# Four of the first layer's weight subtractions issued on GpSimd instead of VectorE

## The chip, the cores and the metric

The kernel runs on one core of a Trainium2 chip. The metric is the device time of one launch in microseconds (us). A core has five engines with instruction queues of their own, each worked through in order: TensorE (PE in the profile, its weight loads PEld), VectorE (DVE), ScalarE (ACT), GpSimd (POOL) and SyncE (SP), which here only starts DMA transfers.

## The reference

Two layers of a bidirectional encoder over 272 tokens (16 meta tokens and 256 others) of width 1024. Each layer normalises its input, multiplies it by one wide matrix, runs retention and attention beside each other on the parts, merges them, and closes with a squared-ReLU MLP:

```
u = rms_norm(h, norm_mix_pre[l])
proj = u @ w_in[l]
q_r, k_r, v_r, g_r, q_a, k_a, v_a, gate_r, gate_a = split(proj)
y_r = retention_branch(q_r, k_r, v_r, g_r, log_decay, pad) @ w_ret_o[l]
y_a = attention_branch(q_a, k_a, v_a, attn_sink[l], pad) @ w_att_o[l]
mix = (sigmoid(gate_r) * y_r + sigmoid(gate_a) * y_a) @ w_mix_o[l]
h = h + rms_norm(mix, norm_mix_post[l])
u = rms_norm(h, norm_ff_pre[l])
h = h + rms_norm(square(relu(u @ w_ff1[l])) @ w_ff2[l], norm_ff_post[l])
```

All is in 32-bit floats. What matters here is the second line, in layer 0.

## The kernel before

The weights come in 260 units of 128 x 1024 floats (512 KB), used in the order in which the program names them. Units 0 to 3 are a special start ("leads": the first four value projections v_r). After them every unit goes the same way (`unit`, from L119): SP fetches it into `raw` (three buffers in rotation, so the DMA for unit n+3 starts when unit n's `raw` has been read by all its readers). ACT rounds it to the matmul's format, `wh` (L131, four buffers). DVE subtracts, `wl = raw - wh` (L132, four buffers), the low part. PE then makes three products for each of eight 128-row slices (`mm3`): `wh` with the activations' high part (L136), `wh` with their low part (L137), `wl` with the high part (L138). So a unit is 24 matmuls of 272 columns, and the third of them is the first that needs `wl`.

The units around the change, all of layer 0, are:

| unit | what it projects | buffers in the rows and the order (raw, wh, wl) |
|---|---|---|
| 4, 5 | values of heads 4 and 5 | wl_296, wl_326 |
| 6 | k_a, the attention keys | raw_113, wh_429, wl_430 |
| 7 | q_a 0, attention queries | raw_475, wh_477, wl_478 |
| 8 | values of head 6 | raw_522, wh_524, wl_525 |
| 9 | q_a 1 | raw_555, wh_557, wl_558 |
| 10 | values of head 7 | raw_602, wh_604, wl_605 |
| 11 | q_a 2 | raw_635, wh_637, wl_638 |
| 12, 13 | v_a, q_a 3 | wl_689, wl_721 |

Between them stand the uses of the products. `value_r` (L416) scales a value product by the norm's factor on DVE (`vt`, L424; two buffers in turn), lets POOL copy its 16 meta columns into a padded tile (`pads`, L427), and defers `centre`: four short PE products of `vt` (L431) and one of `pads` (L432), put into PE's queue in the middle of a later unit, after its fifth slice (`flush` in `product`). For head 6 they stand in the middle of unit 9. `key_a` rotates k_a on DVE (L389 to L392), splits it on ACT (`ka`, four instructions, L449) and DVE (`kal`, L451). `query_a` rotates q_a on DVE, then ACT writes its high part (`qa`, L459, two instructions), DVE its low part (L93, two), and POOL a scaled copy of its meta columns (L465, two).

The order of instructions on each engine is set by the framework's scheduler from its own estimate. The kernel bends it with `tc.issue_after(ins)`: what is traced in that block on the same engine as `ins` goes behind `ins`. `held` is a table from unit number to such instructions, read in `unit`; with an entry that is a POOL instruction only a POOL instruction of the unit is moved.

Of the kernel before, what the change touches and what calls it, by code (L numbers as in the profile page):

```python
# [41 lines left out]
def encoder(ctx: ExitStack, tc: tile.TileContext, order, w, h_in, gains, dec, decm, sink, sinkm, tabs, mats, esel, masks, rel, relm, grow, out):  # L42
    nc = tc.nc
    V, A, PE, G = nc.vector, nc.scalar, nc.tensor, nc.gpsimd
    mul, add, sub, mn = ALU.mult, ALU.add, ALU.subtract, ALU.min
# [27 lines left out]
    def bank(tag, shape=None):  # L73
        t = psum.tile([P, 512], F32, tag=tag, name="ps_" + tag, bufs=BANKS[tag])
        if shape is None:
            return t
        n = int(np.prod(shape))
        v = t[:, :n]
        if len(shape) == 2:
            v = v.rearrange("p (a b) -> p a b", a=shape[0])  # L80
        elif len(shape) == 3:
            v = v.rearrange("p (a b c) -> p a b c", a=shape[0], b=shape[1])
        return v
# [5 lines left out]
    def f(t):  # L89
        return t.bitcast(F32)  # L90
# [13 lines left out]
    count = {"load": 0}  # L104
    raws = []
    held = {}

    def fetch(parts=1):
        i = count["load"]
        count["load"] += 1  # L110
        raw = ring.tile([P, D], F32, tag="raw", name="raw", bufs=3)
        n = D // parts
        cuts = [slice(j * n, (j + 1) * n) for j in range(parts)]
        raws.append((raw, cuts))
        for c in cuts:
            nc.sync.dma_start(raw[:, c], w[i][:, c])
            yield

    def unit(*name):  # L119
        i = len(order)  # L120
        order.append(name)
        if not raws:
            list(fetch())
        raw, cuts = raws.pop(0)
        wh = ring.tile([P, D], F32R, tag="wh", name="wh")
        wl = ring.tile([P, D], F32R, tag="wl", name="wl")
        for c in cuts:
            with ExitStack() as later:
                for ins in held.get(i, ()):
                    later.enter_context(tc.issue_after(ins))  # L130
                A.activation(wh[:, c], raw[:, c], AF.Copy)  # L131
                V.tensor_tensor(out=wl[:, c], in0=raw[:, c], in1=f(wh[:, c]), op=sub)  # L132
        return wh, wl

    def mm3(ps, ah, al, bh, bl, first=True, last=True):
# [6 lines left out]
    def flush():  # L142
        while deferred:
            deferred.pop(0)()

    def product(x, c0, tag, *name):
        wh, wl = unit(*name)
        ps = bank(tag, [T])
        for k in range(KD):
            sl = slice(k * P, (k + 1) * P)  # L150
            ins = mm3(ps[:, c0:], wh[:, sl], wl[:, sl], x[0][:, k, c0:], x[1][:, k, c0:], k == 0, k == KD - 1)
            if k == LAG and deferred:
                with tc.issue_after(ins.ins):
                    flush()
            yield ins, ps

    def proj(x, c0, tag, *name):
        for _, ps in product(x, c0, tag, *name):
            pass
        return ps  # L160
# [177 lines left out]
    def fourfold(x):  # L338
        return x.unsqueeze(1).to_broadcast([x.shape[0], 4, 16])
# [23 lines left out]
    for l in range(DEPTH):  # L363
# [52 lines left out]
        def value_r(hh):  # L416
            q, m = hh // 4, hh % 4
            if m == 0:
                tpv[q] = bank("s", [4, P]), [bank("t") for _ in range(2)]
            tpm, tps = tpv[q]  # L420
            vt = ready.get(hh)
            if vt is None:
                vt = two.tile([P, T], F32, tag="t1", name="vt")
                last = V.scalar_tensor_tensor(out=vt, in0=early.pop(0) if early else proj(u, 0, "a", "v_r", hh), scalar=-0.5, in1=rb, op0=mul, op1=mul)  # L424
                scaled.append(last.ins)
            mine = vtm[:, m]
            G.tensor_copy(mine[:, :, 16 * (m % 2):16 * (m % 2) + 16], fourfold(vt[:, 0:16]))  # L427

            def centre():
                for c in range(2):  # L430
                    PE.matmul(tps[c][:, m * P:(m + 1) * P], vt[:, 16 + c * P:16 + (c + 1) * P], mat["cen"], start=True, stop=True)  # L431
                PE.matmul(tpm[:, m], mine, mat["cen"], start=True, stop=True)  # L432
                if m == 3:
                    for c in range(2):
                        A.activation(vr[:, c, q * 512:(q + 1) * 512], tps[c], AF.Copy)
                    A.activation(vm[:, 4 * q:4 * q + 4], tpm, AF.Copy)
                    for r in odds:
                        low = vm[r, 4 * q:4 * q + 4]
                        V.tensor_tensor(out=low, in0=tpm[r], in1=f(low), op=sub)

            deferred.append(centre)
            if early:
                flush()
# [23 lines left out]
        for hh in range(5):  # L467
            value_r(hh)
# [4 lines left out]
        for i in range(3):  # L473
            value_r(5 + i)
            query_a(i)
# [85 lines left out]
        if l == 0:  # L561
# [6 lines left out]
            for c in range(4):  # L568
                V.tensor_tensor(
                    out=pmblk.rearrange("p (t c g k) -> p t c g k", t=4, c=4, g=2)[:, :, c],  # L570
                    in0=mat["blk"].rearrange("p (t g k) -> p t g k", t=4, g=2),
                    in1=pm[:, 0:16].unsqueeze(1).unsqueeze(1).to_broadcast([P, 4, 2, 16]),
                    op=mul,
# [166 lines left out]
        for m2 in range(4):  # L740
            wh, wl = unit("att_o", m2)
            for i in range(2):
                m = 2 * m2 + i
                ps = bank(wide(), [T])
                for k in range(4):
                    sl = slice((4 * i + k) * P, (4 * i + k + 1) * P)
                    mm3(ps[:, c0:], wh[:, sl], wl[:, sl], ao[:, 0, k, c0:], ao[:, 1, k, c0:], k == 0, k == 3)
                stt(tha[m][:, c0:], tha[m][:, c0:], 1.0, ps[:, c0:], op0=add)
# [47 lines left out]
        if l == 0:  # L796
            def ff2():
                for m in range(KD):
                    ps = bank(wide(), [T])
                    for q in range(4):  # L800
                        wh, wl = unit("ff2", m, q)
                        for k in range(KD):
                            sl = slice(k * P, (k + 1) * P)
                            mm3(ps[:, c0:], wh[:, sl], wl[:, sl], fs[q][0][k][:, c0:], fs[q][1][k][:, c0:], q == 0 and k == 0, q == 3 and k == KD - 1)
                    yield m, ps

            update = leave(l, 3, c0, ff2(), e2)
# [180 lines left out]
```

## Time and profile before

| | |
|---|---|
| median of three runs | 868.79 us (868.16 to 870.78) |
| the profiled execution's own time | 872.21 us |
| its span, first to last instruction | 870.4 us |
| PE busy | 852.1 us, 98% |
| DVE, ACT, POOL busy | 603.2, 559.6 and 49.9 us |
| granted TensorE clock, mean of the span | 0.996 of full |

Read it so: PE has work nearly all the time, so only what leaves PE idle, or slows its clock, can be won or lost. The start up to about 5.7 us, when the first weights land, is not touched by the change. What remains is small, and it has to be looked for by place, not in the averages: in the list of what PE waited for, in the timeline of the stretch from 18 to 45 us, and in the granted clock by stretch.

### The profile page before, as it was taken

The numbers are of one execution on the slowest core, as the hardware profiler recorded it, in microseconds if no ns is written. First come the engines' busy times: TensorE is split into PE (matmuls) and PEld (weight loads), VectorE is DVE, ScalarE is ACT, GpSimd is POOL, SyncE is SP. The second block draws the span as 40 slices with busy tenths as digits, with TensorE's granted clock in tenths as the row PEclk, the third lists the DMA queues.
The fourth block names the chain that finished last, engine by engine and source line by source line (L and its number), as shares of the span: only waits on it lengthen the run. The fifth ranks groups of instructions, "written<-read, shape, count | busy, mean of one in ns | idle before, by whom it ended". The sixth has DMA issues, their size and how long they took to land.

```text
span 870.4 us, 16670 instructions
## 1 busy us (share of the span) xinstructions
PE 852.1 (98%) x6514; PEld 819.3 (94%) x6514; DVE 603.2 (69%) x1113; ACT 559.6 (64%) x1034; POOL 49.9 (6%) x113
## 2 busy tenths in 40 slices
PE   9899999999999999999999999999999999999997
PEld 9899999999989999999989999999999999998885
DVE  7889888778768655444469898888776675554544
ACT  7448887666568777444355588886755498783432
POOL 2112220000000000000000122200000000000000
PEclk9999999999999999999999999999999999999999
DMA  8544344445545655556544544444466367666661
GB/s 294 190 123 136 118 135 131 129 155 173 169 143 171 193 173 183 178 175 186 174 121 146 155 129 154 137 139 137 121 197 198 113 214 204 196 200 192 189 193 69
DMA packets 41407, 142.15 MB, mean 163 GB/s; under 512 B 5360, under 2 KB 6256, under 8 KB 41328
## 3 DMA queue, kind: packets, MB, share of 16 engines
q1 hardware_dynamic: 40896, 140.43, 52.1%
q8 instruction: 51, 0.84, 0.4%
q10 hardware_dynamic: 432, 0.66, 0.2%
q14 instruction: 28, 0.23, 0.1%
HBM read 140.02 MB, written 1.05 MB: 162 GB/s over the span
## 4 chain that ended last, share of the span: by engine, by line
PE 81%; DVE 10%; ACT 6%; issue 1%; DMA 1%; POOL 0%; SPq 0%; DVEq 0%; ACTq 0%; POOLq 0%
PE ps_a L136 12%; PE ps_a L137 12%; PE ps_a L138 12%; PE ps_s L138 5%; PE ps_s L137 5%; PE ps_s L136 5%; PE ps_t L136 4%; PE ps_t L137 4%; PE ps_t L138 4%; DVE wl L132 3%; PE ps_a L849 2%; PE ps_s L849 2%; PE ps_s L848 2%; PE ps_a L848 2%; PE ps_a L850 2%; PE ps_s L850 2%
## 5 line engine op out<-in xcount | busy, mean ns | idle before, releaser
L132 DVE TENSOR_TENSOR wl<-raw,wh 128x1024 fp32r<-128x1024 f32 x256 | 312.8, 1223 | 198.9 <-ACT wh L131 197.3
L131 ACT ACTIVATE wh<-raw 128x1024 fp32r<-128x1024 f32 x256 | 269.9, 1058 | 203.1 <-PE ps_a L137 61.6
L136 PE MATMUL ps_a<-uh,wh 128*128 128x272 f32 (+1 forms) x912 | 265.8, 292 | 2.8 <-ACT uh L242 2.8
L138 PE MATMUL ps_a<-uh,wl 128*128 128x272 f32 (+1 forms) x912 | 259.3, 284 | 0.3 <-DVE wl L132 0.3
L137 PE MATMUL ps_a<-ul,wh 128*128 128x272 f32 (+1 forms) x912 | 259.3, 285 | 0.0
L136 PEld LDWEIGHTS ps_a<-uh,wh 128*128 128x128 f32 x912 | 172.7, 189 | 4.7 <-ACT uh L242 3.2
L137 PEld LDWEIGHTS ps_a<-ul,wh 128*128 128x128 f32 x912 | 172.5, 189 | 0.9
L138 PEld LDWEIGHTS ps_a<-uh,wl 128*128 128x128 f32 x912 | 172.4, 189 | 0.7 <-DVE wl L132 0.7
L138 PE MATMUL ps_s<-uh,wl 128*128 128x272 f32 (+1 forms) x184 | 52.0, 283 | 0.3 <-DVE wl L132 0.3
L137 PE MATMUL ps_s<-ul,wh 128*128 128x272 f32 (+1 forms) x184 | 52.0, 282 | 0.0
L136 PE MATMUL ps_s<-uh,wh 128*128 128x272 f32 (+1 forms) x184 | 52.0, 283 | 0.0
L136 PE MATMUL ps_t<-uh,wh 128*128 128x272 f32 (+1 forms) x152 | 43.2, 284 | 1.3 <-ACT uh L242 1.3
L137 PE MATMUL ps_t<-ul,wh 128*128 128x272 f32 (+1 forms) x152 | 43.1, 284 | 0.0
L138 PE MATMUL ps_t<-uh,wl 128*128 128x272 f32 (+1 forms) x152 | 42.8, 282 | 0.0
L138 PEld LDWEIGHTS ps_s<-uh,wl 128*128 128x128 f32 x184 | 34.6, 188 | 0.5 <-DVE wl L132 0.5
L136 PEld LDWEIGHTS ps_s<-uh,wh 128*128 128x128 f32 x184 | 34.8, 189 | 0.0
L137 PEld LDWEIGHTS ps_s<-ul,wh 128*128 128x128 f32 x184 | 34.7, 189 | 0.0
L136 PEld LDWEIGHTS ps_t<-uh,wh 128*128 128x128 f32 x152 | 28.6, 188 | 1.5 <-ACT uh L242 1.5
L137 PEld LDWEIGHTS ps_t<-ul,wh 128*128 128x128 f32 x152 | 28.6, 188 | 0.1
L138 PEld LDWEIGHTS ps_t<-uh,wl 128*128 128x128 f32 x152 | 28.6, 188 | 0.0
L97 DVE TENSOR_TENSOR fl<-ft,fh 128x272 fp32r<-128x272 f32 (+1 forms) x64 | 27.6, 433 | 1.0 <-ACT fh L96 0.9
L96 ACT ACTIVATE fh<-ft 128x272 fp32r<-128x272 f32 (+1 forms) x64 | 27.1, 424 | 1.7
(308 smaller groups left out, 1948.3 us busy)
## 6 DMA issues: line engine op xcount, KB each, us to landing
raw<-in_w SPq DMA_DIRECT2D x256, 512.0 KB, 3.7
leads<-in_w SPq DMA_DIRECT2D x6, 256.0 KB, 5.3
tab<-in_tabs SPq DMA_DIRECT2D x2, 544.0 KB, 6.5
h<-in_h_in SPq DMA_DIRECT2D x3, 272.0 KB, 5.1
out<-yt SPq DMA_DIRECT2D x3, 256.0 KB, 2.1
leads<-in_w ACTq DMA_DIRECT2D x2, 256.0 KB, 3.8
gj<-in_grow SPq DMA_DIRECT2D x1, 512.0 KB, 5.5
mats<-in_mats SPq DMA_DIRECT2D x1, 320.0 KB, 7.2
```

What stands on the lines that cost most here:

```text
L96: A.activation(xh, x, AF.Copy)
L97: V.tensor_tensor(out=xl, in0=x, in1=f(xh), op=sub)
L131: A.activation(wh[:, c], raw[:, c], AF.Copy)
L132: V.tensor_tensor(out=wl[:, c], in0=raw[:, c], in1=f(wh[:, c]), op=sub)
L136: PE.matmul(ps, ah, bh, start=first, stop=False)
L137: PE.matmul(ps, ah, bl, start=False, stop=False)
L138: return PE.matmul(ps, al, bh, start=False, stop=last)
L848: PE.matmul(pss[i], xh, wh[:, sl], start=kk == 0, stop=False)
L849: PE.matmul(pss[i], xh, wl[:, sl], start=False, stop=False)
L850: PE.matmul(pss[i], xl, wh[:, sl], start=False, stop=kk == KF - 1)
```

## The change

Units 6, 7, 9 and 11 get their subtraction from GpSimd (`G`) where VectorE (`V`) did it. The count of units is `len(order)`, so the set means these units of layer 0 alone; layer 1's units have numbers from 130 on.

```
+    on_pool = {6, 7, 9, 11}
 ...
-                V.tensor_tensor(out=wl[:, c], in0=raw[:, c], in1=f(wh[:, c]), op=sub)
+                (G if i in on_pool else V).tensor_tensor(out=wl[:, c], in0=raw[:, c], in1=f(wh[:, c]), op=sub)
 ...
-            G.tensor_copy(mine[:, :, 16 * (m % 2):16 * (m % 2) + 16], fourfold(vt[:, 0:16]))
+            copied = G.tensor_copy(mine[:, :, 16 * (m % 2):16 * (m % 2) + 16], fourfold(vt[:, 0:16]))
+            if len(order) in on_pool:
+                held[len(order) + 1] = [copied.ins]
```

The last two lines name a POOL copy in `held` for units 7, 8, 10 and 12. Of these only unit 7 has an instruction on POOL, so only its subtraction is kept behind a copy (that of head 4, `vt_424`). Lines behind the first hunk have numbers higher by one in the changed kernel, and by three behind the third.

POOL's queue in the first layer's projections, before (names: `pads` a value's meta columns, `m0` the queries' meta columns; ISA is a switch of POOL's instruction library):

```order
L406 MEMSET m0_383 128x512
L427 COPY pads_355<-vt_392 128x4x16
L427 COPY pads_355<-vt_398 128x4x16
L427 COPY pads_355<-vt5_324 128x4x16
L427 COPY pads_355<-vt_404 128x4x16
L427 COPY pads_355<-vt_410 128x4x16
L427 COPY pads_355<-vt_424 128x4x16
L465 ISA
L465 TENSOR_SCALAR m0_383<-t2_510 64x16 x2
L427 COPY pads_355<-vt_521 128x4x16
```

And after:

```order
L133 ISA
L133 TENSOR_TENSOR wl_430<-raw_113,wh_429 128x1024
L428 COPY pads_355<-vt_392 128x4x16
L428 COPY pads_355<-vt_398 128x4x16
L428 COPY pads_355<-vt_404 128x4x16
L428 COPY pads_355<-vt5_324 128x4x16
L428 COPY pads_355<-vt_410 128x4x16
L428 COPY pads_355<-vt_424 128x4x16
L133 TENSOR_TENSOR wl_478<-raw_475,wh_477 128x1024
L133 TENSOR_TENSOR wl_558<-raw_555,wh_557 128x1024
L133 TENSOR_TENSOR wl_638<-raw_635,wh_637 128x1024
L468 TENSOR_SCALAR m0_383<-t2_510 64x16 x2
```

Unit 6's subtraction stands ahead of the first value copies, right behind the memset of `m0`; the other three stand ahead of the two `m0` instructions, behind which the copy of head 6's value, `vt_521`, still follows. The library switch has moved from behind the copies to ahead of all.

DVE's queue from unit 10's subtraction to head 6's value, before:

```order
L132 TENSOR_TENSOR wl_605<-raw_602,wh_604 128x1024
L392 TENSOR_TENSOR t2_462<-t1_461,t2_462 128x272
L389 TENSOR_TENSOR t1_509<-ps_a_481,tab_283 128x272
L453 COPY m0_383<-t2_462 128x272
L390 STREAM_SHUFFLE t2_510<-t1_509 128x272
L451 TENSOR_TENSOR kal_125<-t2_462,ka_385 64x272
L391 TENSOR_TENSOR t1_509<-ps_a_481,tab_283 128x272
L132 TENSOR_TENSOR wl_638<-raw_635,wh_637 128x1024
L451 TENSOR_TENSOR kal_125<-t2_462,ka_386 64x272
L392 TENSOR_TENSOR t2_510<-t1_509,t2_510 128x272
L424 SCALAR_TENSOR_TENSOR vt_521<-ps_a_528,rb_285 128x272
```

And after (t2_462 is the rotated k_a, t2_510 the rotated q_a 0):

```order
L133 TENSOR_TENSOR wl_605<-raw_602,wh_604 128x1024
L393 TENSOR_TENSOR t2_462<-t1_461,t2_462 128x272
L456 COPY m0_383<-t2_462 128x272
L454 TENSOR_TENSOR kal_125<-t2_462,ka_385 64x272
L390 TENSOR_TENSOR t1_509<-ps_a_481,tab_283 128x272
L391 STREAM_SHUFFLE t2_510<-t1_509 128x272
L454 TENSOR_TENSOR kal_125<-t2_462,ka_386 64x272
L392 TENSOR_TENSOR t1_509<-ps_a_481,tab_283 128x272
L393 TENSOR_TENSOR t2_510<-t1_509,t2_510 128x272
L93 SCALAR_TENSOR_TENSOR qa_387<-t2_510,qa_387 64x272 x2
L425 SCALAR_TENSOR_TENSOR vt_521<-ps_a_528,rb_285 128x272
```

Unit 11's subtraction is gone from it, and the two `qa` instructions now stand ahead of head 6's value instead of behind it.

ACT's queue at the same place, before:

```order
L131 ACTIVATE wh_557<-raw_555 128x1024
L131 ACTIVATE wh_604<-raw_602 128x1024
L131 ACTIVATE wh_637<-raw_635 128x1024
L449 ACTIVATE ka_385<-t2_462 64x272 x2
L449 ACTIVATE ka_386<-t2_462 64x272 x2
L131 ACTIVATE wh_688<-raw_686 128x1024
L459 ACTIVATE qa_387<-t2_510 64x272 x2
```

And after:

```order
L132 ACTIVATE wh_557<-raw_555 128x1024
L132 ACTIVATE wh_604<-raw_602 128x1024
L452 ACTIVATE ka_385<-t2_462 64x272 x2
L452 ACTIVATE ka_386<-t2_462 64x272 x2
L132 ACTIVATE wh_637<-raw_635 128x1024
L462 ACTIVATE qa_387<-t2_510 64x272 x2
L132 ACTIVATE wh_688<-raw_686 128x1024
```

The rounding of unit 11 has moved behind the four `ka` instructions. PE's queue keeps its order but for the order of the short products of the first two values, where the two of `pads` now follow the four of `vt`.

## Rows read from the trace of the kernel before

**Rows 1.** The page, part 1: busy us (share of the span) xinstructions.

```profile
PE 852.1 (98%) x6514; PEld 819.3 (94%) x6514; DVE 603.2 (69%) x1113; ACT 559.6 (64%) x1034; POOL 49.9 (6%) x113
```

**Rows 2.** Waits of PE, 5 to 70 us: us in total, times, longest.

```profile
PE ps_t L431 <- DVE vt L424: 1.2, 1, 1.2
PE ps_s L432 <- POOL pads L427: 1.0, 1, 1.0
PE ps_s L564 <- POOL m L465: 0.6, 1, 0.6
```

**Rows 3.** Windows: us, busy of each engine (xinstructions), granted clock, DMA share.

```profile
44.30:47.60 3.30, 3.30 (x17) 3.30 (x16) 2.23 (x5) 1.06 (x1) 0.00 (x0) 0.50 0.37 142
47.80:51.00 3.20, 3.20 (x27) 3.20 (x27) 1.84 (x6) 1.30 (x2) 0.81 (x3) 1.00 0.57 172
```

**Rows 4.** Timeline, PE: start, us, instruction, count [idle before <-releaser].

```profile
25.32 0.39 PE L432 MATMUL ps_s<-mats,pads 128*128 128x128 f32 x2
...
41.57 0.71 PE L431 MATMUL ps_t<-mats,vt 128*128 128x128 f32 x4 [1.23 <-DVE vt L424]
43.27 0.49 PE L432 MATMUL ps_s<-mats,pads 128*128 128x128 f32 x2 [0.98 <-POOL pads L427]
```

**Rows 5.** The chain that ended last, 30 to 44 us: start, us, what.

```profile
32.73 4.06 DMA raw<-in_w
...
36.90 1.06 ACT wh L131
```

**Rows 6.** Timeline, DVE.

```profile
25.30 0.44 DVE L383 SCALAR_TENSOR_TENSOR vt<-ps_t,rb 128x272 f32<-128x272 f32 x1 [1.61 <-PE ps_t L138]
...
28.06 0.82 DVE L93 SCALAR_TENSOR_TENSOR tab<-tab,rb 128x272 f32<-128x272 f32 x2
28.81 1.21 DVE L132 TENSOR_TENSOR wl<-raw,wh 128x1024 fp32r<-128x1024 f32 x1
...
36.23 0.43 DVE L392 TENSOR_TENSOR t<-t,t 128x272 f32<-128x272 f32 x1
...
41.09 0.43 DVE L424 SCALAR_TENSOR_TENSOR vt<-ps_a,rb 128x272 f32<-128x272 f32 x1
41.44 1.22 DVE L132 TENSOR_TENSOR wl<-raw,wh 128x1024 fp32r<-128x1024 f32 x1
42.68 0.90 DVE L93 SCALAR_TENSOR_TENSOR qa<-t,qa 64x272 fp32r<-64x272 f32 x2
```

**Rows 7.** Timeline, ACT.

```profile
20.32 1.04 ACT L131 ACTIVATE wh<-raw 128x1024 fp32r<-128x1024 f32 x1
...
33.95 1.06 ACT L131 ACTIVATE wh<-raw 128x1024 fp32r<-128x1024 f32 x1 [2.40 <-DMA raw<-in_w]
...
37.86 1.75 ACT L449 ACTIVATE ka<-t 64x272 fp32r<-64x272 f32 x4
```

**Rows 8.** Timeline, POOL; 41.59 is the second of the two L465 there.

```profile
18.26 0.53 POOL L406 MEMSET m<- 128x512 f32 x1 [13.45 <-DVE ss L261]
23.04 0.62 POOL L427 COPY pads<-vt 128x64 f32<-128x64 f32 x2 [4.24 <-DVE vt L424]
...
28.21 0.38 POOL L427 COPY pads<-vt 128x64 f32<-128x64 f32 x1 [0.73 <-DVE vt L424]
...
41.59 1.17 POOL L465 TENSOR_SCALAR m<-t 64x16 f32<-64x16 f32 x1
```

**Rows 9.** POOL's instructions by line: count, duration ns min/median/max, first and last start, forms.

```profile
L465 POOL TENSOR_SCALAR m<-t x8: 245/250/1172, 41.3 to 62.7; 64x16 f32<-64x16 f32 x8
L465 POOLq MODIFY_POOL_CONFIG  x2: 8/8/8, 28.5 to 28.6; - x2
...
L484 POOL COPY vblk<-vat x4: 229/741/1227, 57.0 to 499.9; 64x64 f32<-64x64 f32 x4
...
L594 POOL TENSOR_SCALAR pmk<-ex,rs x32: 437/444/1587, 67.9 to 553.4; 128x64 f32<-128x64 f32 x32
```

**Rows 10.** Groups by form, POOL: count | busy us, mean ns | idle before.

```profile
L329 POOL MEMSET ql<- 128x1088 f32 x1 | 1.0, 1005 | 0.0
```

## The prediction

> **What bounds the kernel now.** I read the busy times first: PE works 98% of the span [rows 1], so time is to be won only where PE stands still or runs slow. The list of what PE waited for between 5 and 70 us has three entries that matter [rows 2], and two of them belong together: at 40.3 us PE is through its fifth slice of unit 9 and wants the short products of head 6's value. `vt` is not there until 41.5, so PE waits 1.23 us; the four products of `vt` start at 41.57, and the two of `pads` wait another 0.98 us, until 43.27 [rows 4]. The granted clock by stretch shows the third part: right after this stall PE runs at 0.50, which is 1.2 GHz, for 3.30 us, and then at 1.00, 2.4 GHz, again [rows 3]. Work of 1.65 us took 3.3, so the fall costs about 1.6 us. The whole prize is 1.2 + 1.0 + 1.6 = 3.8 us, 0.44% of the time.
>
> What ended last before the stall is no lack of DVE work alone: the chain goes through a weight DMA, 32.73 to 36.79, which could start only when DVE had subtracted an earlier unit and so freed its `raw` buffer, and through the rounding on ACT at 36.90 [rows 5]. So the subtractions count twice: for the DVE time that they take, and for when they give a buffer back.
>
> **What is removed.** Four subtractions of 1.21 us each leave DVE [rows 6]: 4.8 us of DVE time. Unit 6's brings nothing by itself: DVE has it done before a wait of 1.61 us for PE [rows 6], which only grows. The other three are in the stretch before the stall.
>
> **What one costs on POOL.** No row shows a subtraction of this size there. Below stands a memset of 1088 columns, one stream written, 1005 ns [rows 10]: 0.92 ns a column, so about 1.0 us. Above stands the scaled copy, L465 with 250 ns for 16 columns and L594 with 444 for 64 [rows 9], 4.0 ns for each further column, so 4.3 us for 1024. I take 2.2 us: it is nearest to the memset, the only long row of POOL, with two input streams read one after the other (2 x 0.94) and a short instruction's 0.25 to start. The Trainium skill, GPSIMD Engine Reference, section 3.1, has a `tensor_tensor` of 2048 floats at 4497 ns, so an estimate of 2.25 us by that page; the sum below would grow by 0.1. No run here shows it yet.
>
> **Who shares the port.** POOL's second L465 starts at 41.59, 0.15 us after a DVE subtraction that runs 41.44 to 42.66 [rows 6, 8], and takes 1.17 us, ending 0.1 us behind it, where the same instruction otherwise takes 0.25 [rows 9]. L484 shows the same, 229 ns or up to 1227 [rows 9]. DVE's subtraction keeps its 1.22 us. So POOL cannot read while DVE runs an instruction with two inputs in SBUF. The other direction, DVE behind a long POOL read, is in no row, since POOL's are all short. I take it as the same, with 0 and the whole 2.2 us as its bounds. The Trainium skill, SBUF — State Buffer, section Who interferes with whom, states the pair as exclusive both ways, for a whole instruction, whichever starts first; it speaks against this change, since each subtraction on POOL then shuts DVE's out for longer than DVE needed for it. The rows bear out the one half.
>
> **Unit 6.** `wh` is done at 20.32 + 1.04 = 21.36 [rows 7]. POOL is free from 18.8 [rows 8] and ends at about 23.6; the first two value copies, at 23.04 before [rows 8], come 1 us later, at 24.1. PE needs them at 25.32 [rows 4], so the cover is 1.2 us and the cost nothing.
>
> **Unit 7.** It is behind the copy at 28.21 to 28.59 [rows 8] and then behind DVE's two `tab` instructions, until 28.88 [rows 6]: 28.88 + 2.2 = 31.1, against 28.81 + 1.21 = 30.02 on DVE [rows 6]. At 0.12 us a matmul [rows 3], unit 9 began 15 matmuls ahead of the stall at 40.3, near 38.4, and unit 7 another 48 and six short products ahead of that, near 32, so PE doesn't wait. But unit 7's `raw` comes free 1.1 us later, and it is the buffer of unit 10. Before, unit 10's rounding began at 33.95, after a wait for its DMA [rows 7], 3.93 us after the release; now 31.1 + 3.9 = 35.0.
>
> **The new wait.** Unit 10's subtraction stays on DVE, and in DVE's queue it stands ahead of k_a's last rotation step, `kal`, q_a 0's rotation and head 6's `vt`. All of them are queued behind a subtraction that waits for `raw`. The rotation step moves from 36.23 [rows 6] to 37.3 and ends at 37.75. ACT's four `ka` take 1.75 us [rows 7], to 39.5; unit 11's rounding, now behind them, 1.06 us [rows 7], to 40.5. POOL then subtracts unit 11, 40.5 to 42.7. ACT's `qa` follow that rounding, and DVE's two `qa`, now ahead of `vt`, read two SBUF inputs: they wait for the port until 42.7, take 0.90 [rows 6] and end at 43.6. `vt` is done at 44.0 (41.52 before), and PE's four short products begin at 44.05. POOL has only 0.5 us of `m0` and a copy of 0.24 left by then, so the `pads` products start 0.45 behind, at 44.5. Before: 43.27 [rows 4]. **Sum: +1.2 us.** Unit 9's subtraction is done on POOL behind DVE's unit 8, by about 34.7, and PE needs it near 38.5: cost nothing, cover over 3 us.
>
> Since units 7 and 11 both stand on this chain, each further microsecond of the subtraction costs two: 1.0 us gives 1.2 - 2.4 = -1.2, and 4.3 us gives +5.4. If DVE doesn't wait for POOL, `vt` is done at 42.2, but the copy is still behind POOL's own subtraction (42.7 + 0.5 + 0.3 = 43.5): +0.2. The clock has fallen after a stall of 3 us; after one of 4 I take one fall too, at the same price. Bounds: 1.6 less if none comes, 1.6 more if two do.
>
> Behind the stall the order of the queues is as before, and PE's wait for L465 at 63 us, the third of its entries [rows 2], hangs on work that starts from PE's own products, so it moves along and gives nothing back.
>
> **Against which time.** The profiled execution took 872.21 us for a span of 870.4; the three runs have a median of 868.79. A stall shift of 1.2 us is the same in both, so the forecast is 868.8 + 1.2 = **870.0 us**. A measurement of this kernel can tell about 0.3%, 2.6 us, from no change.
>
> **The rivals.**
> *Long subtractions (slower).* The one mechanism is the length on POOL, through the two links above. From 1.2 + 2 x (t - 2.2) > 2.6 it decides beyond t = 2.9 us; at 3.1 us the time is 868.8 + 3.0 = 871.8. For it: the scaled copy's 4 ns a column, and that POOL has to contend with DVE. Against: the memset's rate.
> *The library switch.* It took 8 ns in the list [rows 9], but before it stood at 28.5 with POOL's next instruction due at 41.3 [rows 9], so up to 12.7 us were hidden; now the next one is due 2.6 us after 18.8. If what it sets off takes L, unit 6's subtraction starts at 18.8 + L, and the two copies are late for PE (about 26.0, behind the four `vt` products) from L = 4.5 on. At half the hidden time, L = 6.3, that is 1.8 us, together 868.8 + 1.2 + 1.8 = 871.8; at most 8.2 us. The Trainium skill, GPSIMD Engine Reference, section 2.1, has about 6 us for the first call of a freshly loaded kernel, with no row of its own; by it the stall would be 1.5 us. No row here shows any part of it.
> *A second fall of the clock.* 870.0 + 1.6 = 871.6.
> *DVE not held up, 2.2 us.* +0.2: 869.0.
> *Short subtractions (faster).* At 1.2 us, with DVE not held up, unit 7 is done at 30.1 as before, ACT has unit 11 rounded at 39.6, `vt` is done at 41.25 and `pads` at 41.7: 1.5 us won, and if the clock then stays up 1.6 more, 868.8 - 3.1 = 865.7. For it: DVE loses 3.6 us of work ahead of `vt`. Against: the queue behind unit 10's `raw`.
> That the change doesn't do what it says is out: the order of the queues shows the four subtractions on POOL. That the hold does nothing for units 8, 10 and 12 costs nothing, as no instruction there moves.
>
> **Chances.** Forecast 0.43 (within); DVE not held up 0.08 (within); long subtractions 0.16, library 0.11, second fall 0.06 (slower, 0.33 in all); short subtractions 0.16 (faster). So 0.16 faster, 0.51 the same, 0.33 slower. The range leaves out half of the fast rival and the upper part of the long subtractions: 866.5 to 873.0.
>
> **What would show it.** Right: POOL rows of about 2.2 us for the four; unit 10's rounding at about 35; DVE idle ahead of unit 10's subtraction; the `qa` instructions on DVE starting as POOL ends unit 11; `pads` products at about 44.5, a slow stretch behind them. Wrong: POOL rows away from 2.2 us, each 0.1 us worth 0.2; PE idle near 26 us (the switch); DVE's `qa` running beside POOL's subtraction; `vt_521` before 41.5; a clock of 1.00 throughout from 44 us.

## The result and the profile after

The changed kernel takes 874.25 us (median of 20 runs, 872.58 to 878.32) beside 870.25 us for the kernel before (20 runs, 867.76 to 873.66). The ratio is 1.0052 with a 95% interval of 1.0039 to 1.0064: 4.5 us slower, 3.4 to 5.6. The forecast was 870.0 us, 1.2 us slower, with a range that ended at 873.0. The profiled execution took 873.45 us for a span of 871.7, at a mean granted clock of 0.995.

The waits of PE from 5 to 70 us (us in total, times, longest) answer [rows 2]; the two waits for head 6's value have become one of 4.1 us:

```profile
PE ps_t L434 <- DVE vt L425: 4.1, 1, 4.1
PE ps_s L567 <- POOL m L468: 0.6, 1, 0.6
```

PE's timeline (start, us, instruction, idle before and its releaser) and two windows (us, busy of PE, PEld, DVE, ACT, POOL, granted clock, DMA share, GB/s) answer [rows 4] and [rows 3]:

```profile
44.22 1.23 PE L434 MATMUL ps_t<-mats,vt 128*128 128x128 f32 x4 [4.12 <-DVE vt L425]
45.44 0.79 PE L435 MATMUL ps_s<-mats,pads 128*128 128x128 f32 x2
```

```profile
44.30:47.60 3.30, 3.30 (x13) 3.00 (x14) 0.99 (x1) 0.00 (x0) 1.09 (x1) 0.50 0.73 220
47.80:51.00 3.20, 3.20 (x19) 3.20 (x18) 2.61 (x6) 1.06 (x1) 0.00 (x0) 0.63 0.13 54
```

The four products of `vt` took 0.71 us before and take 1.23 now: PE comes out of the longer wait already at 0.50, 1.2 GHz, and is still there in the first part of the second window, where before it was back at 1.00. One more window of the changed kernel shows that the clock fell while PE still stood:

```profile
43.40:44.20 0.80, 0.00 (x0) 0.00 (x0) 0.77 (x3) 0.00 (x0) 0.39 (x1) 0.50 0.57 82
```

What made `vt` late stands in three timelines. ACT and POOL (answering [rows 7, 8]):

```profile
34.83 1.06 ACT L132 ACTIVATE wh<-raw 128x1024 fp32r<-128x1024 f32 x1 [3.52 <-DMA raw<-in_w]
37.54 1.77 ACT L452 ACTIVATE ka<-t 64x272 fp32r<-64x272 f32 x4 [1.64 <-DVE t L393]
39.33 1.06 ACT L132 ACTIVATE wh<-raw 128x1024 fp32r<-128x1024 f32 x1
```

```profile
21.20 2.40 POOL L133 TENSOR_TENSOR wl<-raw,wh 128x1024 fp32r<-128x1024 f32 x1 [2.65 <-ACT wh L132]
...
28.32 2.59 POOL L133 TENSOR_TENSOR wl<-raw,wh 128x1024 fp32r<-128x1024 f32 x1
31.39 2.96 POOL L133 TENSOR_TENSOR wl<-raw,wh 128x1024 fp32r<-128x1024 f32 x1 [0.48 <-ACT wh L132]
40.46 2.46 POOL L133 TENSOR_TENSOR wl<-raw,wh 128x1024 fp32r<-128x1024 f32 x1 [6.11 <-ACT wh L132]
42.90 0.91 POOL L468 TENSOR_SCALAR m<-t 64x16 f32<-64x16 f32 x2
44.30 1.09 POOL L428 COPY pads<-vt 128x64 f32<-128x64 f32 x1 [0.49 <-DVE vt L425]
```

and DVE (answering [rows 6]):

```profile
35.92 1.23 DVE L133 TENSOR_TENSOR wl<-raw,wh 128x1024 fp32r<-128x1024 f32 x1 [2.35 <-ACT wh L132]
37.07 0.43 DVE L393 TENSOR_TENSOR t<-t,t 128x272 f32<-128x272 f32 x1
...
41.22 2.47 DVE L93 SCALAR_TENSOR_TENSOR qa<-t,qa 64x272 fp32r<-64x272 f32 x2 [0.49 <-ACT qa L462]
43.72 0.44 DVE L425 SCALAR_TENSOR_TENSOR vt<-ps_a,rb 128x272 f32<-128x272 f32 x1
44.08 1.22 DVE L133 TENSOR_TENSOR wl<-raw,wh 128x1024 fp32r<-128x1024 f32 x1
```

Read down: unit 10's rounding waits for its DMA until 34.83; DVE stands still for 2.35 us ahead of unit 10's subtraction, and k_a's last step (L393, 37.07) is queued behind it; ACT's `ka` wait for that step, unit 11's rounding waits behind the `ka`, and POOL subtracts unit 11 from 40.46 to 42.92. DVE's two `qa` start at 41.22 and end at 43.69, 2.47 us for what took 0.90 [rows 6], and `vt` is behind them. Last, the copy of head 6 on POOL takes 1.09 us beside DVE's subtraction at 44.08. The loss is in this one stretch, but which of its links makes it, the profile alone doesn't tell.

To compare runs I use the **local shift**: the start of the same matmul of PE's queue at 90 us, after the last stall, less that of before, and less the difference that the two had already at 24 us (it comes from when the first weights land). For the changed kernel: 2.67 + 0.24 = 2.91 us. It is read from one profile of each kernel, the ratio from all runs.

### The profile page after: what moved, and what is told of

Same layout as the page of the kernel before. It is cut to its first block, busy times and chain, and to the rows that moved or that the text cites. A ratio compares the mean times of both kernels' runs of the same rounds, so it can differ in the third digit from the quotient of the medians.

```text
span 871.7 us, 16668 instructions
## 1 busy us (share of the span) xinstructions
PE 851.1 (98%) x6514; PEld 818.0 (94%) x6514; DVE 602.4 (69%) x1109; ACT 560.0 (64%) x1034; POOL 60.3 (7%) x117
## 4 chain that ended last, share of the span: by engine, by line
PE 80%; DVE 10%; ACT 6%; issue 2%; DMA 1%; POOL 0%; SPq 0%; DVEq 0%; ACTq 0%; POOLq 0%
PE ps_a L138 12%; PE ps_a L137 12%; PE ps_a L139 12%; PE ps_s L139 5%; PE ps_s L138 5%; PE ps_s L137 5%; PE ps_t L137 4%; PE ps_t L138 4%; PE ps_t L139 4%; DVE wl L133 3%; PE ps_a L852 2%; PE ps_s L852 2%; PE ps_s L851 2%; PE ps_a L851 2%; PE ps_a L853 2%
## 5 line engine op out<-in xcount | busy, mean ns | idle before, releaser
L133 DVE TENSOR_TENSOR wl<-raw,wh 128x1024 fp32r<-128x1024 f32 x252 | 308.2, 1224 | 199.7 <-ACT wh L132 198.4
```

The lines of the kernel that those rows point to most:

```text
L133: (G if i in on_pool else V).tensor_tensor(out=wl[:, c], in0=raw[:, c], in1=f(wh[:, c]), op=sub)
```

## The experiments

All are run beside the kernel before; "against before" is the ratio to it, less one, times 870 us, with the 95% interval.

| run | on POOL | against before, us | local shift, us |
|---|---|---|---|
| the change | 6, 7, 9, 11 | +4.5 (3.4 to 5.6) | +2.91 |
| nohold | 6, 7, 9, 11 | +4.7 (3.0 to 6.4) | +3.2 |
| s679 | 6, 7, 9 | +2.2 (0.7 to 3.7) | +0.76 |
| s6911 | 6, 9, 11 | +0.1 (-1.4 to 1.6) | -0.07 |
| s69 | 6, 9 | -3.8 (-5.1 to -2.5) | -4.09 |
| only9 | 9 | -2.6 (-4.1 to -1.2) | -3.36 |
| after_rot | 6, 7, 9, 11 | +0.6 (-0.6 to 1.9) | +0.61 |
| after_vt | 6, 7, 9, 11 | +1.0 (-0.3 to 2.5) | +0.06 |
| after_rot_vt | 6, 7, 9, 11 | -2.5 (-4.0 to -1.0) | -3.24 |
| s679_rot | 6, 7, 9 | +0.3 (-1.1 to 1.8) | -0.25 |
| before_rot | none | -2.4 (-3.7 to -1.2) | -3.41 |
| before_warm | none | -2.5 (-3.7 to -1.3) | -1.29 |
| after_warm | 6, 7, 9, 11 | +1.1 (-0.3 to 2.4) | +0.66 |

### Which unit: s69, s679, s6911

```
-    on_pool = {6, 7, 9, 11}
+    on_pool = {6, 9}            # s69
+    on_pool = {6, 7, 9}         # s679
+    on_pool = {6, 9, 11}        # s6911
```

> Only units 6 and 9 are subtracted by GpSimd; 7 and 11 are back on VectorE. Theory T (two links and the clock): the loss is made by unit 7, whose late subtraction gives its raw buffer back late and so holds VectorE's queue behind unit 10's subtraction, and by unit 11, behind which VectorE's qa wait for the port; units 6 and 9 cost nothing. Then unit 10's rounding is back at 33.9 us or a little earlier, vt_521 is done at 41.0 to 41.6, the pads products start at 42.5 to 43.3, the slow stretch of the clock is again about 3.3 us, and the time is 0 to 0.5 us under the kernel before. Rival R (every long subtraction on GpSimd shuts VectorE out for its length): the four cost the same, some 0.8 to 1.1 us each, so +1.6 to +2.2 us here. Rival U (unit 6's first subtraction, after GpSimd's change of library and beside the skn instruction that took 1.70 us, is the cause): the whole +3.2 to +4.5 us stays.

> Units 6, 7 and 9 by GpSimd, 11 by VectorE. T: unit 10's rounding stays at about 34.8 us, k_a's last step at about 37.1, so ACT rounds unit 11 at 39.3 as in the changed kernel; VectorE then has unit 11's subtraction ahead of or beside its qa (1.2 us instead of a wait of 2.5), vt_521 is done at 43.0 to 44.0, the stall ends at 43.3 to 44.5, and the time is 1.5 to 2.5 us over the kernel before. Rival C (unit 11 alone makes the loss, through the port): within 0.5 us of the kernel before. Rival R: +2.4 to +3.4 us.

> Units 6, 9 and 11 by GpSimd, 7 by VectorE. T: unit 10's rounding is back at 33.9 us, ACT rounds unit 11 at 38.4 or earlier, GpSimd subtracts it till about 41, the two qa on VectorE wait for that, vt_521 is done at 41.5 to 42.3 and the pads products start at 42.5 to 43.5: the time is within 0.6 us of the kernel before, so that unit 11 costs little without unit 7 ahead of it. Rival C (unit 11 alone makes the loss): all of it stays, +3.2 to +4.5 us. Rival R: +2.4 to +3.4 us.

The three rivals fall: each of the four costing the same (R) needs a loss with units 6 and 9, and unit 6 as the cause (U) too, but s69 is 3.8 us under the kernel before. Unit 11 alone (C) needs the whole loss in s6911, which is at +0.1. Theory T has s679 and s6911 in its ranges by the ratio (s679's local shift, 0.76, is under its 1.5 to 2.5), but by it s69 only gets back to the kernel before, and there it missed by 3.5 us. In s69 (PE's waits, timeline, window):

```profile
PE ps_s L567 <- POOL m L468: 0.7, 1, 0.7
```

```profile
40.24 0.71 PE L434 MATMUL ps_t<-mats,vt 128*128 128x128 f32 x4
40.79 0.39 PE L435 MATMUL ps_s<-mats,pads 128*128 128x128 f32 x2
```

```profile
44.30:47.60 3.30, 3.30 (x30) 3.30 (x28) 3.23 (x7) 2.02 (x4) 0.94 (x3) 1.00 0.57 174
```

No wait for `vt`, no fall of the clock: all of the prize of 3.8 us that the prediction named is there to be had. DVE's timeline of s69 shows why, and it is nothing that T spoke of:

```profile
34.06 1.06 DVE L393 TENSOR_TENSOR t<-t,t 128x272 f32<-128x272 f32 x1
35.15 0.30 DVE L456 COPY m<-t 128x272 f32<-128x272 f32 x1
35.37 1.22 DVE L133 TENSOR_TENSOR wl<-raw,wh 128x1024 fp32r<-128x1024 f32 x1
...
39.75 0.43 DVE L425 SCALAR_TENSOR_TENSOR vt<-ps_a,rb 128x272 f32<-128x272 f32 x1
40.10 0.43 DVE L393 TENSOR_TENSOR t<-t,t 128x272 f32<-128x272 f32 x1
```

k_a's last step stands ahead of unit 10's subtraction, where before and in the changed kernel it stands behind; and `vt` stands ahead of q_a 0's last step. The build sets the order of a queue by its own estimates, so here a change of what is on POOL changed the order on DVE. In s6911 k_a's step is ahead too (34.20), but `vt` is behind q_a 0's step and its `qa`, as in the changed kernel. That gave a new theory, Q: two places in DVE's queue make the loss.

### The place of k_a's step: after_rot, before_rot

```
+    steps = []
 ...
+                if i == 10:
+                    later.enter_context(tc.issue_after(steps[0]))
                 (G if i in on_pool else V).tensor_tensor(out=wl[:, c], ...)
 ...
-            V.tensor_tensor(out=t2[:, sl], in0=t1[:, sl], in1=t2[:, sl], op=add)
+            steps.append(V.tensor_tensor(out=t2[:, sl], in0=t1[:, sl], in1=t2[:, sl], op=add).ins)
```

> The changed kernel with all four units on GpSimd, but k_a's last rotation step (t, L393 of the changed kernel) put ahead of unit 10's subtraction in VectorE's queue, as it already stands in the runs with units 6 and 9 and with 6, 9 and 11. Theory Q (the place in the queue): what unit 7 costs is that this step stands behind a subtraction which waits for a late raw buffer; with the step ahead of it, ka is done near 37 us instead of 39.3, ACT rounds unit 11 near 37 to 38, GpSimd has it by 40.5 instead of 42.9, vt_521 is done at 42.3 to 43.2, and the time is 0 to 1.2 us over the kernel before, so 3 us or more under the changed kernel. Rival B (the late buffer itself): unit 10's rounding stays near 34.8 us and delays what follows whatever the place of the step; the time stays at +3 to +5 us.

> The kernel before, nothing on GpSimd, only k_a's last rotation step put ahead of unit 10's subtraction in VectorE's queue. Q: ka is done about 1 us earlier than 39.6, vt_521 done at 40.3 to 41.5, PE's stall at 40.3 us falls from 1.2 + 1.0 to 0 to 1.2 in all and the clock may stay up: 1 to 4 us under the kernel before, without any work on GpSimd. Rival V (it is the VectorE time that the subtraction of unit 9 takes, and not the order, that made the run with units 6 and 9 fast): within 0.6 us of the kernel before.

before_rot has the same edit in the kernel before. Q holds, B and V fall. In after_rot the buffer is as late as ever, but nothing of k_a waits for it (ACT):

```profile
35.04 1.06 ACT L133 ACTIVATE wh<-raw 128x1024 fp32r<-128x1024 f32 x1 [3.46 <-DMA raw<-in_w]
36.01 1.75 ACT L455 ACTIVATE ka<-t 64x272 fp32r<-64x272 f32 x4
37.78 1.06 ACT L133 ACTIVATE wh<-raw 128x1024 fp32r<-128x1024 f32 x1
```

Unit 11 is rounded 1.5 us earlier and the local shift falls from 2.91 to 0.61. before_rot has not one subtraction on POOL and wins 2.4 us. This isn't the place of k_a's step alone: in this build's order `vt` (40.01) has also moved, from behind q_a 0's last step to ahead of it (41.83), so both places are mended there. Of its waits this is left of 1.2 + 1.0:

```profile
PE ps_t L434 <- DVE vt L427: 0.2, 1, 0.2
```

### The place of `vt`: after_vt, after_rot_vt

In both, q_a 0's last step, its four `qa` (two on ACT, two on DVE) and its two `m0` instructions are issued after `vt_521`; after_rot_vt has the edit of after_rot as well.

```
-            r = rotated(proj(u, c0, "a", "q_a", t), 2, XOR8, c0)
-            for a in range(2): ...
+            r = rotated(proj(u, c0, "a", "q_a", t), 2, XOR8, c0, hold=l == 0 and t == 0)
+            def rest(): ...                    # last step, qa, m0
 ...
                 scaled.append(last.ins)
+                if queued:
+                    with tc.issue_after(last.ins):
+                        queued.pop()()
```

> The changed kernel with all four units on GpSimd, but head 6's vt (vt_521) put back ahead of q_a 0's last rotation step and its qa in VectorE's queue, where it stands in the kernel before; k_a's step stays behind unit 10's subtraction. Theory Q (the loss is made by two places in VectorE's queue, not by the subtractions themselves): vt is done at about 40.3 us instead of 44.1, before GpSimd starts unit 11, and PE's first products start there; the pads copy still stands behind unit 11's subtraction on GpSimd and comes at 42.9 to 43.4 us. The time is within 0.8 us of the kernel before, some 4 us under the changed kernel. Rival P (the port: GpSimd's subtractions cost VectorE what they take, wherever vt stands): +3 to +5 us stays.

> The changed kernel with all four units on GpSimd and both places in VectorE's queue mended: k_a's last rotation step ahead of unit 10's subtraction, vt_521 ahead of q_a 0's last step. Q: unit 11 is rounded by 38.9 and subtracted on GpSimd by 41.4, the copy behind it is done at 41.7, the pads products start at 41.6 to 42 us, and the clock stays up or falls for less: 1.5 to 3.5 us under the kernel before, 6 us or more under the changed kernel, although the same four subtractions run on GpSimd. Rival P: it stays where the run with the rotation step alone was, at +0.6 us, or above.

Q holds again and P falls. In after_vt `vt` is done at 40.98 and no longer waits for POOL, but the copy of head 6 is behind unit 11's subtraction (43.15), so the stall ends about where it ended in the kernel before (`pads` products at 43.65, before at 43.27); its +1.0 is just over the 0.8 expected. The edit reaches POOL's queue too: the copy now stands ahead of the two `m0`. With both places mended the four subtractions are still on POOL, and the time is 2.5 us under the kernel before. PE, DVE and POOL of after_rot_vt:

```profile
39.93 0.70 PE L445 MATMUL ps_t<-mats,vt 128*128 128x128 f32 x4
41.42 0.49 PE L446 MATMUL ps_s<-mats,pads 128*128 128x128 f32 x2 [0.79 <-POOL pads L439]
```

```profile
39.43 0.43 DVE L433 SCALAR_TENSOR_TENSOR vt<-ps_a,rb 128x272 f32<-128x272 f32 x1
39.78 1.49 DVE L397 TENSOR_TENSOR t<-t,t 128x272 f32<-128x272 f32 x1
```

```profile
38.59 2.38 POOL L136 TENSOR_TENSOR wl<-raw,wh 128x1024 fp32r<-128x1024 f32 x1 [4.24 <-ACT wh L133]
40.92 0.45 POOL L439 COPY pads<-vt 128x64 f32<-128x64 f32 x1
```

The port still holds DVE up: q_a 0's step takes 1.49 us instead of 0.43 and ends at 41.27, 0.3 us behind POOL's subtraction. It costs nothing there, since `vt` is past it.

### Unit 7 with the step in its place, and unit 9 alone: s679_rot, only9

s679_rot is after_rot with `on_pool = {6, 7, 9}`, only9 the changed kernel with `on_pool = {9}`.

> Units 6, 7 and 9 on GpSimd with k_a's last rotation step ahead of unit 10's subtraction; the same step stands there in the run with 6 and 9, so that unit 7 on GpSimd is what differs. Q: unit 10's rounding is at about 35 us, unit 11's at about 37.8, VectorE subtracts it till 40.1, vt is done at 41.2 to 41.6 and the pads copy near 43: within 0.6 us of the kernel before, 1 to 3 us under the run with 6, 7 and 9 without the step ahead, and 3 to 4 us over the run with 6 and 9. If unit 7 costs nothing once the step is in its place, it is 3 to 4 us under the kernel before.

> Unit 9 alone on GpSimd. VectorE's queue around 34 to 42 us stands as in the run with units 6 and 9. If unit 6 costs and gains nothing, as the prediction has it, the time is that of the run with 6 and 9: 3 to 4.5 us under the kernel before, no wait of PE at 40 us, the clock at 1.00. If the 1.2 us of VectorE that unit 6 frees near 22 us are needed for it, the stall comes back in part and the time is 0 to 2 us under the kernel before.

s679_rot came out as Q has it, 3.8 us of local shift above s69: unit 10 is a microsecond later, unit 11's subtraction, ahead of `vt` in both, starts at 38.91 instead of 38.27, and in this build's order `vt` is also behind q_a 0's step (40.50), and the copy of head 6 behind two `m0` instructions (1.50 us for both, beside DVE's subtraction at 41.21), where in s69 it is ahead of them. So the order changed once more, and what unit 7 costs by itself stays open. only9 wins 2.6 us, between its two forecasts (3 to 4.5 and 0 to 2): unit 9 alone brings most of what 6 and 9 bring. The intervals of s69 and only9 overlap, so whether unit 6 adds anything stays open.

### The clock: before_warm, after_warm

Extra matmuls of a zero tile in PE's queue, just ahead of head 6's short products, ten in before_warm and twenty in after_warm (each is two instructions in the profile); they add work and leave nothing out.

```
                 with tc.issue_after(ins.ins):
+                    if len(order) == 10:
+                        warm(10, "o")        # 20 in after_warm
                     flush()
```

> The kernel before with ten extra matmuls of a zero tile, about 0.23 us each by the ones at 683.8 us, in PE's queue where it waits at 40.3 us, ahead of head 6's short products. They delay nothing that is ready before 42.6 us and the pads products are due at 43.27. What is left out by them is the fall of the clock: the granted clock stays at 1.00 from 44.3 to 47.6 us, and the time is 1.6 us under the kernel before. If the fall does not come from PE standing still, the clock falls all the same and the time is that of before.

> The changed kernel with twenty such extra matmuls, 4.5 us, in PE's queue where it waits at 40.1 us. The wait for vt and pads itself stays: the pads products start at 45.2 to 45.6 us. The clock stays at 1.00, which gives back the 5.9 us at half rate: 2 to 2.9 us under the changed kernel, so 1 to 2.5 us over the kernel before. Against before_warm that is the loss without the clock, 2.2 to 2.6 us; if the loss were the clock's alone, after_warm and before_warm would be the same.

The clock stays at 1.00 in both. Before_warm and after_warm in the window of [rows 3]:

```profile
44.30:47.60 3.30, 3.30 (x29) 3.30 (x28) 2.36 (x5) 1.06 (x1) 0.00 (x0) 1.00 0.38 143
```

```profile
44.30:47.60 3.30, 2.97 (x25) 2.78 (x25) 1.51 (x3) 0.40 (x1) 1.10 (x1) 1.00 0.56 197
```

The extra matmuls do not put off the `pads` products: in both, these wait for POOL's copy. Before_warm and after_warm:

```profile
43.48 0.49 PE L434 MATMUL ps_s<-mats,pads 128*128 128x128 f32 x2 [0.63 <-POOL pads L429]
```

```profile
45.63 0.49 PE L437 MATMUL ps_s<-mats,pads 128*128 128x128 f32 x2 [0.33 <-POOL pads L430]
```

What the clock costs is read behind them. From the start of the `pads` products to the same later matmul of PE's queue (at 52.1 us in the kernel before) PE needs 8.82 us before and 7.18 in before_warm, 9.33 in the changed kernel and 7.17 in after_warm. So the fall costs 1.64 us before, which is the prediction's 1.6, and 2.16 after. Of the change's 2.91 us of local shift the clock is 0.5; the other 2.4 are the later products, 45.44 + 0.24 against 43.27. Before_warm's local shift, -1.29, is smaller than the 1.64 because its products come 0.37 us later than before, counted from the weights: unit 10's rounding waits for its DMA until 34.34 there, 33.95 before.

The clock stayed up as both expectations have it, and after_warm's products are within its range to 0.03 us. The times were further down than forecast, 2.5 us under before instead of 1.6 and 3.4 under the changed kernel instead of 2 to 2.9, but inside what the intervals allow.

### The hold: nohold

```
-            if len(order) in on_pool:
-                held[len(order) + 1] = [copied.ins]
```

> The changed kernel without the hold of units 8, 10 and 12 behind a value copy. On GpSimd unit 7's subtraction then stands ahead of the copy of head 4 (vt_424) and not behind it; nothing else moves. T: unit 7 is subtracted up to 0.5 us earlier, but behind it the copies come later, head 6's copy still waits for VectorE's subtraction of unit 12; the time is that of the changed kernel, +3 to +5 us against the kernel before. A rival by which the hold itself made the loss (unit 8, 10 and 12 kept back) has it at 0 to +1.5 us.

The hold is no cause: without it the loss is the same. But more changed than was expected, and the loss comes by another way. Unit 7's subtraction now runs from 27.44 to 29.82, a microsecond earlier, so its buffer is back in time and unit 10's rounding starts at 33.58, earlier than in the kernel before. Instead DVE is held beside POOL: its two `tab` take 2.45 us instead of 0.82, and unit 8's subtraction ends a microsecond behind POOL's at 31.62:

```profile
31.97 3.13 DVE L133 TENSOR_TENSOR wl<-raw,wh 128x1024 fp32r<-128x1024 f32 x1
```

Unit 10's subtraction follows at 36.47 and k_a's step at 37.61, about where they are in the changed kernel. So a late buffer is not the only thing that makes this stretch late: here DVE, held beside POOL's subtractions, does it in its place.

## Why the prediction was wrong

**What bounds the kernel, and the prize**: right. The kernels without the stall (s69, only9, before_rot) win 3.4 to 4.1 us by local shift; the prize was put at 3.8, and its clock part of 1.6 measured 1.64.

**The subtraction on POOL**, 2.2 us: 2.35 to 2.40 where DVE leaves it alone (21.20; 40.85 in after_vt), 2.59 where DVE's `tab` pair still runs as it starts (28.32), up to 3.34 where DVE's subtraction runs first (s69, 31.48). The estimate of 2.25 us from the Trainium skill, GPSIMD Engine Reference, section 3.1, is 4 to 6% under the trace's 2.35 to 2.40.

**The port in both directions**: right. DVE's first `qa` start at 41.22 with their inputs there, and the pair takes 2.47 us beside POOL's 40.46 to 42.92. This is the half that no row before showed. The Trainium skill, SBUF — State Buffer, section Who interferes with whom, states it so, and the trace agrees.

**Unit 6 and the library switch**: right. POOL starts unit 6 at 21.20, 0.08 us behind ACT's rounding (20.08 + 1.04), and PE does not wait near 26 us. The rival of the switch falls.

**The new wait, link by link**: unit 10's rounding at 34.83 (forecast 35.0), DVE idle for 2.35 us ahead of the subtraction, k_a's step at 37.07 (37.3), unit 11 rounded till 40.39 (40.5), POOL till 42.92 (42.7), `vt` done at 44.16 (44.0). This chain was right to 0.3 us, or to 0.5 once the 0.24 by which the changed run had its weights earlier are counted, and the runs confirm its links: after_rot and after_vt each take one away, and the loss falls to what can't be told from zero (+0.6 and +1.0).

**The step that failed is the sum behind `vt`.** It had the `pads` products 0.45 us behind the first product of `vt`, at 44.5; they start 1.22 behind, at 45.44, or at 45.63 where the clock is kept up. "POOL has only 0.5 us of `m0` and a copy of 0.24 left by then" left out that DVE starts unit 12's subtraction at 44.08, right behind `vt`, and that the copy has to wait for it: 1.09 us instead of 0.24. The very thing stood in the rows of before, at the `m0` instruction of 41.59 [rows 8]. In the changed kernel PE shows no wait for the copy, since its four products of `vt` at half rate end as the copy does (45.45 and 45.39); after_warm, at full clock, shows the copy alone: PE waits 0.33 us for it. With `vt` itself 0.16 us later (0.40, once the 0.24 of the weights are counted) the products are late by 2.41 us, not 1.2.

**The clock was mis-sized.** The prediction's "after one of 4 I take one fall too, at the same price" took the price for a constant. The half rate lasts from 43.4 or earlier to 50.1 us, about twice as long as before, and costs 2.16 us, not 1.6. The prediction held that outcome as a rival of its own, a second fall, with 0.06 and 1.6 us more, and did not add it to the others. It cost 0.5 more: its first 0.8 us or more passed while PE stood, and the slower products of `vt` ran while the copy was not done.

Together 2.91 us instead of 1.2. The measured 4.5 us (from 3.4) is more than the trace's 2.91; what the rest is, is not settled. One candidate is the fall itself. Of the 99 runs of the kernel before that stand beside the experiments, 39 have a mean granted clock of 0.998 or 0.999, which no profile with a fall in this stretch has (0.995 to 0.997), and they are 1.2 to 2.1 us shorter on average than the others; of the changed kernel's 20 runs none is above 0.997. So the kernel before seems to go without the fall in many runs, though not in the profiled one, and the changed kernel in none. No run tests this. In absolute time the forecast missed by 4.25 us, and 1.46 of them are its base: 868.79 was the median of three runs, the twenty have 870.25.

**The rivals.** None of the five happened as priced; the second fall came, at 0.5 instead of 1.6. Long subtractions named a loss of 3.0 us, near the 2.91, but that is chance: its one cause was the length, and that was 2.35 to 2.59 on the two links, under its point of 2.9. What was missing is the question that s69 answers: the two places in DVE's queue were both read in the prediction ("All of them are queued behind a subtraction that waits for `raw`"; "`qa`, now ahead of `vt`"), but as given. With both moved the loss is gone: the same four subtractions win 2.5 us, and before_rot wins as much with none. What POOL itself gives, beyond the order, is not above what these runs can tell: after_rot_vt and before_rot are at 0.9971 and 0.9972. The lowest ratio is that of s69, 0.9956 (0.9941 to 0.9971), and its interval overlaps those of after_rot_vt, only9 and before_rot.

## What to carry to other kernels

Where a build orders the queues, a step taken off an engine changes who stands ahead of whom on it: look in the order for a short instruction that others wait for behind one that waits for a buffer or a port, and move that first, before any work. In these runs work on GpSimd cost VectorE nothing where VectorE's instructions beside it took an input from PSUM, or were ones that nobody waited for. When a stall of PE grows, work out the clock's share anew from the stretch behind it: here it grew from 1.64 to 2.16 us as the stall went from 3 us to 5. Then ask what else ends late beside the step that you price, as DVE's next subtraction did here beside a copy of 0.24 us.

## What the runs showed of the hardware beside that

A DVE instruction with a single input in SBUF was held too. This 128x16 `TENSOR_SCALAR` starts inside POOL's first subtraction (21.20 to 23.60) and ends with it; before, and in only9, where unit 6 is on DVE, it took 0.16 us:

```profile
21.93 1.70 DVE L357 TENSOR_SCALAR skn<-sk 128x16 f32<-128x16 f32 x1
```

The stream shuffle at 32.62, beside unit 9's subtraction, was not (0.47 us as before), nor were DVE's instructions with an input in PSUM (`t` L390 and L392, `vm` L442).

In the second half of the kernel matmuls run at one of two paces at the full granted clock and with PE never idle. The first line is before, the second the changed kernel, the same window:

```profile
636.00:676.00 40.00, 40.00 (x342) 40.00 (x341) 28.93 (x46) 22.11 (x34) 0.00 (x0) 1.00 0.68 212
```

```profile
636.00:676.00 40.00, 40.00 (x356) 40.00 (x355) 30.59 (x49) 22.38 (x34) 0.00 (x0) 1.00 0.69 213
```

342 matmuls in 40 us are 117 ns each, 356 are 112 ns. In nohold's profile, a kernel with the loss too, the slow pace stands at 715 to 755 us instead (342 there, 356 in before), where no kernel of this study differs. Of the fourteen profiles before and before_warm have it in the first of these windows, nohold and before_rot in the second, the other ten in neither: all three kernels without a subtraction on POOL, and one of eleven with. What sets it is not known. In the profiles of before and of the change it gives the changed kernel some 2 us back, which is why the spans differ by 1.3 us only. If it comes in some executions and not in others, it would add to the spread between runs; whether it does, one profile of each kernel can't say. In these two it lengthens the kernel before, so it can't be the rest of the 4.5 us by what they show.
